# Queries and keys of two head pairs split at full height with halves placed by DMA, and attention bias tiles loaded by query half

## The chip, the core and the metric

The kernel runs on one core of a Trainium2 chip. A core has five engines that each work through their own list of instructions in order: TensorE (PE) for matrix products, VectorE (DVE), ScalarE (ACT) and GpSimd (POOL) for element-wise work, and SyncE (SP), which here only issues DMAs. They meet through semaphores. The metric is the device time of one execution in microseconds (us), the median of several runs.

## What is computed

Two layers of a diffusion backbone on 512 latent tokens (a grid of 8 rows by 64 columns) and 256 context tokens, model width 1024, everything in float32. Layer 0 has two groups of eight heads side by side: latent attention (MLA) and neighbourhood attention, then a SwiGLU block. Layer 1 has sliding-window attention and a SwiGLU block. The change concerns the neighbourhood heads of layer 0 alone. What they compute, cut to the core:

```python
def na_heads(q, k, v, qc, kc, vc, rel_bias, ctx_out):
    ...
    def row(args):
        r, qr = args
        rs = jnp.clip(r - kr // 2, 0, n_rows - kr)
        k_blk = lax.dynamic_slice_in_dim(kg, rs, kr, axis=1)[:, :, kcol]
        v_blk = lax.dynamic_slice_in_dim(vg, rs, kr, axis=1)[:, :, kcol]
        s_lat = jnp.einsum('bnqhd,bknmhd->bhnqkm', qr, k_blk).astype(jnp.float32) * scale
        s_lat = s_lat + col_bias[:, dr_idx].transpose(0, 2, 3, 1, 4)[None]
        s_lat = jnp.where(col_ok[:, :, None, :], s_lat, NEG_INF).reshape(b, h, n_cb, NA_CB, kr * NA_KB)
        s_ctx = jnp.einsum('bnqhd,bchd->bhnqc', qr, kc).astype(jnp.float32) * scale
        p = jax.nn.softmax(jnp.concatenate([s_ctx, s_lat], axis=-1), axis=-1).astype(v.dtype)
    ...
```

Each latent query reads the latent keys of a 16-column neighbourhood, with a learned bias, and all context keys, in one softmax; context queries read context keys.

## The kernel before

Activations lie transposed: features on the 128 partitions, the 768 tokens (512 latent, 256 context) along the free dimension. Two heads of width 64 share a tile, one in partitions 0 to 63 and one in 64 to 127; the eight neighbourhood heads are four such pairs, 0 to 3.

TensorE works in a rounded float32 type (fp32r). To keep full accuracy a value x is split into a high part, its cast to fp32r, and a low part, x minus the high part. For the scores (`stacked_scores`, L754) each head needs one query tile with the high part in one half of the partitions and the low part in the other, and two key tiles that hold the high part of the keys twice, and the low part twice. Two matmuls over all 128 partitions then give high times high plus low times high, and the rest.

`put_q` (L716) and `put_k` (L731) make these tiles. For pairs 0 and 1 they run straight out of the projection. For pairs 2 and 3 the projections first put the raw queries and keys into tiles of tag `p` (the list `raws`), and `split_pair` (L1032) makes the tiles later, as side work while pairs 0 and 1 are attended. For each of the two heads apart, on 64 partitions at a time: the query's high part is a cast (L723, on ScalarE), its low part a subtraction (L724, on GpSimd), which writes straight into the other half of the partitions; the keys' high part is a cast (L737, on VectorE for pair 2, on ScalarE for pair 3), the low part a subtraction on VectorE (L738), and a DMA copies each to the other half (L740 and L741, through the helper at L136). The tables `RK`, `RQ` and `RL` (L61) choose these engines. The tiles of pair 2 have tag `b`, those of pair 3 tag `st`.

The attention is a chain of jobs (`pair_jobs`, L637): for a pair first the context queries (blocks 4 and 5), then the latent query blocks 0 and 1 of both heads, then 2 and 3. In a job each head in turn has its scores made into a PSUM buffer of tag `s`, of which there are three; `take` (L567, VectorE) adds the bias, writes the negated scores to SBUF and keeps the extreme; `exps` (L563, ScalarE) takes the exponential and its sum. Then `turned` (L505 and on) transposes the probabilities on TensorE (L511), copies them out of PSUM (L502, VectorE, or L503, ScalarE), and `weighted` (L557) multiplies with the values. `attend` interleaves the front of one job with the back of the one before and with side work: the split, the norms of the MLA group (`gained`: squares on GpSimd L990, sums L997, roots L1000, gains on VectorE L977), later its projections (L346 to L349). While the first pair starts, VectorE, GpSimd and ScalarE still finish modulation sums (L240, L257, L258).

The bias of one head is two tiles of 128x768 of tag `nb`: tile 0 serves query blocks 0 and 1, tile 1 blocks 2 and 3. Tag `nb` has two buffers, so a third tile can be loaded only when the first is done with. `nb_tiles` (L953) issues both loads of a head when the pair's jobs are built, head after head.

The final order on each engine is made by a scheduler that simulates the program when it is built, with priorities from the order in which it is written. So an edit can move instructions around it. All DMAs named here are issued from SP, in one order: an issue that waits holds up those behind it.

## Time and profile before

| | |
|---|---|
| Timed runs | 1573.1, 1574.36, 1575.22 us; median 1574.36 |
| The profiled execution | 1578.6 us, its span 1576.8 |
| Mean granted TensorE clock | 0.993 |
| Neighbourhood attention begins, ends | about 177 us, about 262 us |

The profile follows one execution. Busy time counts what an engine executes; a wait is put down to what released it. `pss`, `pst`, `psd`, `pso` are PSUM tiles of the tags `s`, `t`, `d`, `o`. Where all DMAs of SP stand at L136, they are told apart by their tiles. Within the edited stretch the engines are busy as follows (us in each 20 us; the last three numbers are granted clock, share of the DMA engines, GB/s):

```profile
160.00:180.00 20.00, 19.45 (x117) 17.14 (x115) 15.64 (x35) 9.74 (x23) 13.19 (x11) 1.00 0.16 38
180.00:200.00 20.00, 17.57 (x121) 14.00 (x120) 15.23 (x39) 15.90 (x43) 13.66 (x9) 0.91 0.46 128
200.00:220.00 20.00, 17.93 (x131) 14.50 (x130) 15.23 (x40) 17.81 (x41) 4.63 (x5) 0.91 0.45 129
220.00:240.00 20.00, 19.50 (x150) 15.54 (x150) 15.86 (x37) 14.59 (x34) 7.45 (x5) 1.00 0.35 106
240.00:260.00 20.00, 19.53 (x150) 16.17 (x149) 16.24 (x40) 14.85 (x38) 9.57 (x8) 1.00 0.24 65
```

The columns are the stretch, its length, and the busy time of PE, of its weight loads, of DVE, ACT and POOL, each with its count of instructions.

### The profile page before, as it was taken

The numbers are of one execution on the slowest core, as the hardware profiler recorded it, in microseconds if no ns is written. First come the engines' busy times: TensorE is split into PE (matmuls) and PEld (weight loads), VectorE is DVE, ScalarE is ACT, GpSimd is POOL, SyncE is SP. The second block draws the span as 40 slices with busy tenths as digits, with TensorE's granted clock in tenths as the row PEclk, the third lists the DMA queues.
The fourth block names the chain that finished last, engine by engine and source line by source line (L and its number), as shares of the span: only waits on it lengthen the run. The fifth ranks groups of instructions, "written<-read, shape, count | busy, mean of one in ns | idle before, by whom it ended". The sixth has DMA issues, their size and how long they took to land.

```text
span 1576.8 us, 26525 instructions
## 1 busy us (share of the span) xinstructions
PE 1529.3 (97%) x10016; PEld 1372.7 (87%) x10016; DVE 1174.8 (75%) x2346; ACT 796.1 (50%) x1607; POOL 276.3 (18%) x302
## 2 busy tenths in 40 slices
PE   6999999999999999999999999999999999999998
PEld 4787778887998999999998988877889999899998
DVE  3885777685878587686858676879976778678685
ACT  4563677775465243242423335558856545354453
POOL 0144724320111101102111132470012000000001
PEclk9999999999999999999999999999999999999999
DMA  9645242004654444647466485110225133323322
GB/s 318 249 131 174 79 127 76 11 7 160 207 168 144 151 167 162 219 126 272 157 198 229 144 325 185 54 41 2 69 76 164 54 97 125 99 89 128 84 97 88
DMA packets 76463, 214.90 MB, mean 136 GB/s; under 512 B 9872, under 2 KB 16400, under 8 KB 76336
## 3 DMA queue, kind: packets, MB, share of 16 engines
q1 hardware_dynamic: 59216, 144.42, 28.1%
q0 software_dynamic: 15968, 67.24, 12.3%
q8 instruction: 78, 1.28, 0.3%
q10 hardware_dynamic: 1152, 1.57, 0.3%
q14 instruction: 49, 0.40, 0.1%
HBM read 186.97 MB, written 23.07 MB: 133 GB/s over the span
## 4 chain that ended last, share of the span: by engine, by line
PE 77%; DVE 10%; DMA 6%; ACT 3%; issue 2%; POOL 0%; SPq 0%; DVEq 0%; ACTq 0%; POOLq 0%
PE pso L557 5%; PE pss L1392 5%; PE pss L1391 5%; PE pss L1390 4%; PE psd L346 4%; PE psd L349 4%; PE psd L348 4%; PE pss L346 4%; PE pss L349 4%; PE pss L348 3%; PE pst L1392 3%; PE pst L1390 3%; PE pst L1391 3%; PE pst L346 3%; PE pst L348 3%; PE pst L349 3%
## 5 line engine op out<-in xcount | busy, mean ns | idle before, releaser
L335 ACT CAST wh<-wr 128x1024 fp32r<-128x1024 f32 (+2 forms) x148 | 115.5, 795 | 208.2 <-DMA wr<-in_w_dn_dram 48.9
L336 DVE TENSOR_TENSOR wl<-wr,wh 128x1024 fp32r<-128x1024 f32 (+2 forms) x145 | 133.0, 924 | 81.1 <-ACT wh L335 79.5
L563 ACT ACTIVATE p<-p,sm 128x512 f32<-128x512 f32 (+3 forms) x144 | 104.9, 729 | 28.5 <-DVE sm L567 26.7
L1390 PE MATMUL pss<-b,wh 128*128 128x384 f32 (+1 forms) x346 | 108.0, 313 | 0.6 <-ACT b L372 0.6
L1391 PE MATMUL pss<-b,wh 128*128 128x384 f32 (+1 forms) x346 | 108.2, 313 | 0.1
L1392 PE MATMUL pss<-b,wl 128*128 128x384 f32 (+1 forms) x346 | 107.3, 312 | 0.0
L348 PE MATMUL psd<-b,wh 128*128 128x512 f32 (+3 forms) x262 | 89.6, 342 | 0.0
L302 DVE CUSTOM_DVE_ANT_0 p<-rope,cond 128x1024 bf16<-128x1024 f32 x64 | 76.9, 1221 | 11.3 <-DMA rope<-in_mod_w_dram 11.2
L292 POOL DMA_DIRECT2D rope<-in_mod_w_dram x48 | 25.7, 535 | 321.1 <-DVE mod L302 308.7
L346 PE MATMUL psd<-b,wh 128*128 128x512 f32 (+3 forms) x222 | 80.0, 361 | 0.9 <-ACT b L476 0.6
L557 PE MATMUL pso<-ph,b 128*64 128x256 f32 (+1 forms) x384 | 78.9, 365 | 0.4 <-DVE ph L502 0.4
L349 PE MATMUL psd<-b,wl 128*128 128x512 f32 (+3 forms) x222 | 78.7, 355 | 0.0
L557 PE MATMUL pso<-pl,b 128*64 128x256 f32 (+1 forms) x384 | 78.5, 363 | 0.0
L1390 PE MATMUL pst<-b,wh 128*128 128x384 f32 (+1 forms) x226 | 70.7, 313 | 2.5 <-DVE p L1229 1.9
L1392 PE MATMUL pst<-b,wl 128*128 128x384 f32 (+1 forms) x226 | 70.7, 313 | 1.4 <-DVE wl L1378 1.4
L1391 PE MATMUL pst<-b,wh 128*128 128x384 f32 (+1 forms) x226 | 70.5, 312 | 0.0
L1377 ACT CAST wh<-pl 128x512 fp32r<-128x512 f32 x78 | 44.9, 620 | 50.0 <-PE pss L1391 22.6
L348 PE MATMUL pss<-b,wh 128*128 128x256 f32 (+3 forms) x216 | 69.2, 321 | 0.0
L1377 ACT CAST wh<-wr 128x1024 fp32r<-128x1024 f32 x39 | 41.0, 1051 | 54.5 <-PE pst L1391 14.6
L346 PE MATMUL pss<-st,wh 128*128 128x512 f32 (+2 forms) x198 | 67.1, 339 | 0.3 <-ACT wh L335 0.3
L349 PE MATMUL pss<-st,wl 128*128 128x512 f32 (+2 forms) x198 | 67.2, 339 | 0.1
L1390 PEld LDWEIGHTS pss<-b,wh 128*128 128x128 f32 x346 | 65.9, 191 | 1.1 <-ACT b L372 0.9
(627 smaller groups left out, 5377.6 us busy)
## 6 DMA issues: line engine op xcount, KB each, us to landing
wr<-in_w_gu_dram SPq DMA_DIRECT2D x88, 512.0 KB, 4.1
rope<-in_mod_w_dram POOLq DMA_DIRECT2D x48, 512.0 KB, 3.9
wr<-in_w_dn_dram SPq DMA_DIRECT2D x73, 256.0 KB, 3.0
wr<-in_w_out_dram SPq DMA_DIRECT2D x32, 512.0 KB, 4.0
p<-home POOLq DMA_DIRECT2D x40, 384.0 KB, 5.4
home<-p POOLq DMA_DIRECT2D x40, 384.0 KB, 5.4
wr<-in_w_in_dram SPq DMA_DIRECT2D x21, 512.0 KB, 4.4
nb<-in_nb_dram SPq DMA_DIRECT2D x16, 384.0 KB, 3.2
```

The source lines that it names most:

```text
L302: behind(V.tensor_tensor_reduce(out=T("p", [P, D], mybir.dt.bfloat16), in0=w, in1=cond[:, v, :], op0=ALU.mult, op1=ALU.add, scale=1.0, sca ...
L335: behind(S.copy(h, r), *after[:1])
L336: behind((G if eng else V).tensor_tensor(lo, r, f(h), op=ALU.subtract), *after[1:])
L346: ins = PE.matmul(o, wh[:, k], mh[:, c], start=first and k == 0, stop=False)
L348: PE.matmul(o, wh[:, k], ml[:, c], start=False, stop=False)
L349: PE.matmul(o, wl[:, k], mh[:, c], start=False, stop=last and k == n - 1)
L557: ins = PE.matmul(o[64 * i : 64 * i + 64, c], v(kt), t, start=n == 0, stop=n == len(moving[i]) - 1)
L563: S.activation(p[:, c], p[:, c], AF.Exp, bias=nm, scale=-1.0, accum_out=dn)
L1377: S.copy(h, t)
L1390: PE.matmul(o, wh, xh, start=first and k == 0, stop=False, skip_group_check=not first)
L1391: PE.matmul(o, wh, xl, start=False, stop=False, skip_group_check=not first)
L1392: PE.matmul(o, wl, xh, start=False, stop=k == 3, skip_group_check=not first)
```

## The change

Two edits. First, `split_pair` no longer calls `put_q` and `put_k`. The queries of both heads are cast in one instruction over all 128 partitions (ScalarE) and subtracted in one (VectorE, the low part written over the raw tile); the keys likewise. What has to lie in another half of the partitions is then placed by DMAs: three for the queries, six for the keys. Some of these overwrite what others read, so they wait for one another. Second, `nb_tiles` takes a pair and loads the tiles by query half: first head's tile 0, second head's tile 0, first head's tile 1, second head's tile 1.

```diff
-RK, RQ, RL, SQ = (2, 0), (0, 0), (0, 0), 1
+SQ = 1
...
-    def nb_tiles(h):
-        ts = [T("nb", [P, NT]) for i in range(2)]
+    def nb_tiles(p):
+        ts = {}
         for i in range(2):
-            dma(ts[i], I["nb"][h, i])
+            for s in range(2):
+                ts[s, i] = T("nb", [P, NT])
+                dma(ts[s, i], I["nb"][2 * p + s, i])
         cut = (slice(0, 512), slice(256, 768), slice(256, 768), slice(0, 512))
-        return lambda n: ts[n // 2][:, cut[n]]
+        return [lambda n, s=s: ts[s, n // 2][:, cut[n]] for s in range(2)]
...
-        how = S.copy, G.tensor_copy, V.tensor_copy
         sets.append((new_q(tag), new_k(tag)))
-        put_q(sets[p][0], None, how[RQ[p - 2]], (G, V)[RL[p - 2]].tensor_tensor)(q, slice(0, NT))
+        up, dn = slice(0, 64), slice(64, 128)
+        t0, t1 = sets[p][0]
+        S.copy(t0[:, :NT], q)
+        lo = q.bitcast(F32R)
+        V.tensor_tensor(lo, q, f(t0[:, :NT]), op=ALU.subtract)
         yield
-        put_k(sets[p][1], KC[1], how[RK[p - 2]])(k, slice(0, NT))
+        dma(t1[up, :NT], t0[dn, :NT])
+        dma(t1[dn, :NT], lo[dn])
+        dma(t0[dn, :NT], lo[up])
+        (h0, l0), (h1, l1) = sets[p][1]
+        S.copy(h0[:, :NT], k)
+        V.tensor_tensor(l0[:, :NT], k, f(h0[:, :NT]), op=ALU.subtract)
+        yield
+        for x, y in ((h0, h1), (l0, l1)):
+            dma(y[up, :NT], x[dn, :NT])
+            dma(y[dn, :NT], x[dn, :NT])
+            dma(x[dn, :NT], x[up, :NT])
         yield
...
-            hs = []
+            hs, near = [], nb_tiles(p)
...
-                hs.append(Head(..., None, nb_tiles(2 * p + s), -LOWEST, sums, mins))
+                hs.append(Head(..., None, near[s], -LOWEST, sums, mins))
```

In the built program GpSimd has four instructions fewer, VectorE and ScalarE two fewer each, SP ten DMAs more, and TensorE the same 9416 in a partly other order. Engine orders differ only between the start of the first pair's attention and the start of the MLA heads, and in one swap of neighbours far behind.

Where pair 2 is split, VectorE's order was this (L240 and L244 belong to a modulation sum; the `ISA` rows of L567 are takes, with `zeros` for context blocks and `nb` for bias tiles, and the row behind each reads its accumulator):

```order
L737 CAST b_1855<-p_1563 64x768
L240 ISA p_1786,mod_293_1376<-pl_1784,cond_66,mod_293_1376 128x512
L240 ISA mod_293_1376 128x1
L738 TENSOR_TENSOR b_1856<-p_1563,b_1855 64x768
L737 CAST b_1857<-p_1563 64x768
L244 SCALAR_TENSOR_TENSOR mod_293_1376<-mod_293_1376,modb_89 128x1
L567 ISA p_1834,sm_1824<-pss_1833,zeros_95 128x256
L567 ISA sm_1824 128x1
L567 ISA p_1844,sm_1824<-pss_1843,zeros_95 128x256
L567 ISA sm_1824 128x1
L738 TENSOR_TENSOR b_1858<-p_1563,b_1857 64x768
L567 ISA p_1876,sm_1824<-pss_1871,nb_1825 128x512
```

and with the change it is this (L1043 subtracts the queries, L1050 the keys):

```order
L240 ISA p_1786,mod_293_1376<-pl_1784,cond_66,mod_293_1376 128x512
L240 ISA mod_293_1376 128x1
L1043 TENSOR_TENSOR p_1478<-p_1478,b_1853 128x768
L244 SCALAR_TENSOR_TENSOR mod_293_1376<-mod_293_1376,modb_89 128x1
L1050 TENSOR_TENSOR b_1856<-p_1563,b_1855 128x768
L567 ISA p_1834,sm_1824<-pss_1833,zeros_95 128x256
L567 ISA sm_1824 128x1
L567 ISA p_1844,sm_1824<-pss_1843,zeros_95 128x256
L567 ISA sm_1824 128x1
L567 ISA p_1871,sm_1824<-pss_1866,nb_1825 128x512
```

Two instructions for four, and none is left between the context takes and the first bias take.

On SP, at the same place, four key copies stood ahead of the bias loads before. `nb_1829` is the first head's tile 1 afterwards and the second head's tile 0 before. A wait for a `DMAHW` counter is one for an earlier DMA:

```order
L136 DMA b_1855<-b_1855 64x768 [waits DMAHW5_49,DVE_49]
L136 DMA b_1856<-b_1856 64x768 [waits DMAHW6_49,DVE_49]
L136 DMA b_1857<-b_1857 64x768 [waits DMAHW7_49,DVE_49]
L136 DMA b_1858<-b_1858 64x768 [waits DMAHW0_49,DVE_49,PE_49]
L136 DMA nb_1829<-in_nb_dram 128x768 [waits DMAHW1_49,DVE_49]
L136 DMA nb_1830<-in_nb_dram 128x768 [waits DMAHW2_49,DMAHW1_49,DVE_49]
L136 DMA nb_2000<-in_nb_dram 128x768 [waits DMAHW3_49,DVE_49]
```

and with the change:

```order
L136 DMA b_1854<-b_1853 64x768 [waits DMAHW5_49,PE_49,Activation_49]
L136 DMA b_1857<-b_1855 64x768 [waits DMAHW6_49,PE_49,Activation_49]
L136 DMA b_1854<-p_1478 64x768 [waits DMAHW7_49,DVE_49]
L136 DMA b_1853<-p_1478 64x768 [waits DMAHW5_49,DMAHW0_49]
L136 DMA b_1857<-b_1855 64x768 [waits DMAHW1_49]
L136 DMA b_1858<-b_1856 64x768 [waits DMAHW2_49,DVE_49,PE_49]
L136 DMA b_1858<-b_1856 64x768 [waits DMAHW3_49]
L136 DMA b_1855<-b_1855 64x768 [waits DMAHW6_49,DMAHW4_49,DMAHW1_49]
L136 DMA nb_1829<-in_nb_dram 128x768 [waits DVE_49]
L136 DMA b_1856<-b_1856 64x768 [waits DMAHW3_49,DMAHW2_49]
L136 DMA nb_1831<-in_nb_dram 128x768 [waits DMAHW7_49,DVE_49]
```

Eight copies now stand ahead of the first bias reload, which is called A1 below, and one behind it; the fourth waits for the first, the eighth for the second and the fifth.

On ScalarE, behind the first context exponentials, the order with the change is this (L258 is a modulation sum, L503 a copy out of PSUM, L1041 the fourth pair's query cast; `p_1934` is the exponential that needs A1):

```order
L563 ACTIVATE p_1871,sm_1823<-p_1871,sm_1824 128x512
L563 ACTIVATE p_1834,sm_1823<-p_1834,sm_1824 128x256
L563 ACTIVATE p_1844,sm_1823<-p_1844,sm_1824 128x256
L258 ACTIVATE ph_1780,part_1801<-ph_1780 128x512
L563 ACTIVATE p_1895,sm_1823<-p_1895,sm_1824 128x512
L258 ACTIVATE pl_1784,part_1804<-pl_1784 128x512
L563 ACTIVATE wr_1913,sm_1823<-wr_1913,sm_1824 128x512
L563 ACTIVATE p_1924,sm_1823<-p_1924,sm_1824 128x512
L503 COPY ph_1886<-psd_1881 128x512
L1041 CAST st_2162<-p_1647 128x768
L563 ACTIVATE p_1934,sm_1823<-p_1934,sm_1824 128x512
```

Before, the first L258 stood ahead of the first of these rows, both PSUM copies ahead of the second head's exponentials, and between them and the exponential in the last row stood three casts.

## The prediction

> **What bounds the kernel now.** I read the page's first part, then the chain that ended last, then the stretches around the edited stage, then single instructions there. The page:

> ```profile
> span 1576.8 us, 26525 instructions
> PE 1529.3 (97%) x10016; PEld 1372.7 (87%) x10016; DVE 1174.8 (75%) x2346; ACT 796.1 (50%) x1607; POOL 276.3 (18%) x302
> PE 77%; DVE 10%; DMA 6%; ACT 3%; issue 2%; POOL 0%; SPq 0%; DVEq 0%; ACTq 0%; POOLq 0%
> ```

> TensorE is busy 97% of the span and carries 77% of the chain. No edit removes a matmul, so only time in which TensorE stands, or runs at a lower clock, can be won. The edits act between about 176 us (the first split) and about 260 us (the last bias tile). Busy time by stretch (columns: length, then PE, PEld, DVE, ACT, POOL; then the granted clock, DMA share, GB/s):

> ```profile
> 177.50:260.00 82.50, 76.47 (x558) 61.77 (x558) 64.96 (x159) 65.37 (x156) 37.69 (x28) 0.96 0.38 108
> 260.00:280.00 20.00, 20.00 (x153) 16.33 (x155) 12.83 (x39) 14.59 (x34) 7.02 (x8) 1.00 0.27 78
> ```

> TensorE stands for 82.50 - 76.47 = 6.0 us in this stretch, and behind it it is full again, so what is won there should be kept. The waits of that stretch (total, times, longest):

> ```profile
> PE pss L757 <- DVE sm L567: 3.0, 5, 0.9
> PE psd L511 <- DVE b L977: 1.5, 1, 1.5
> ```

> Half of it is score matmuls waiting for VectorE's `take` (L567) to free one of three PSUM buffers; a quarter is one wait for the gain multiplies. The clock adds to it:

> ```profile
> 182.00:184.00 2.00, 2.00 (x16) 2.00 (x16) 1.11 (x6) 2.00 (x7) 1.92 (x2) 0.84 0.45 98
> 184.00:186.00 2.00, 2.00 (x12) 2.00 (x11) 0.00 (x0) 0.93 (x4) 1.86 (x2) 0.50 0.63 194
> 186.00:188.00 2.00, 1.98 (x14) 1.68 (x14) 1.39 (x3) 0.77 (x2) 1.99 (x2) 0.80 0.01 3
> 214.00:216.00 2.00, 2.00 (x8) 1.21 (x8) 2.00 (x6) 2.00 (x5) 2.00 (x2) 0.52 0.00 2
> 216.00:218.00 2.00, 2.00 (x11) 1.34 (x10) 1.20 (x5) 2.00 (x6) 1.79 (x4) 0.62 0.54 133
> ```

> Twice the clock falls to half for about 3.4 us, each time right behind a group of waits. The first costs 2 x (0.16 + 0.50 + 0.20) = 1.7 us, the second 2 x (0.48 + 0.38) = 1.7 us. So the **most** that can be won is 6.0 + 3.4 = 9.4 us.

> **The split of the third pair.** VectorE and TensorE at its place:

> ```profile
> 176.74 1.14 DVE L738 TENSOR_TENSOR b<-p,b 64x768 fp32r<-64x768 f32 x1
> 177.91 0.65 DVE L737 CAST b<-p 64x768 fp32r<-64x768 f32 x1
> 178.58 0.24 DVE L244 SCALAR_TENSOR_TENSOR mod<-mod,modb 128x1 f32<-128x1 f32 x1
> 178.75 0.41 DVE L567 CUSTOM_DVE_ANT_0 p<-pss,zeros 128x256 f32<-128x256 f32 x1
> 179.54 1.45 DVE L738 TENSOR_TENSOR b<-p,b 64x768 fp32r<-64x768 f32 x1
> 181.02 0.69 DVE L567 CUSTOM_DVE_ANT_0 p<-pss,nb 128x512 f32<-128x512 f32 x1
> 179.22 0.39 PE L757 MATMUL pss<-st,st 128*128 128x256 f32 x1 [0.55 <-DVE sm L567]
> 180.10 0.33 PE L511 MATMUL pst<-ident_r,p 128*128 128x128 f32 x1
> 180.59 0.33 PE L511 MATMUL psd<-ident_r,p 128*128 128x128 f32 x1 [0.16 <-ACT p L563]
> 181.78 0.36 PE L757 MATMUL pss<-st,st 128*128 128x192 f32 x1 [0.85 <-DVE sm L567]
> ```

> The second subtraction (1.45 us) stands between the context takes and the first bias take; TensorE waits 0.85 us for that take, and 0.55 us for the one before. What the new operations cost follows from instructions of the same kinds and widths:

> ```profile
> 175.37 1.68 ACT L723 CAST b<-p 64x768 fp32r<-64x768 f32 x2
> 208.76 0.83 ACT L372 CAST b<-b 128x768 fp32r<-128x768 f32 x1
> L738 DVE TENSOR_TENSOR st<-p,st 64x768 fp32r<-64x768 f32 x2 | 1.9, 948 | 0.0
> 211.06 0.95 DVE L373 TENSOR_TENSOR b<-b,b 128x768 fp32r<-128x768 f32 x1
> L724 POOL TENSOR_TENSOR b<-p,b 64x768 fp32r<-64x768 f32 x2 | 4.2, 2116 | 0.2
> L724 POOL TENSOR_TENSOR st<-p,st 64x768 fp32r<-64x768 f32 x2 | 3.6, 1818 | 0.5 <-ACT st L723 0.4
> ```

> A cast of 128x768 takes 0.83 us, as one of 64x768 does (1.68 for two), and a subtraction 0.95 us at either height: twice the partitions are free. Third pair: VectorE loses two casts and two subtractions and gains two subtractions, ScalarE keeps two casts, GpSimd loses 4.2 us. Fourth pair: VectorE keeps two subtractions, ScalarE has two casts for four (1.7 us less), GpSimd loses 3.6 us. GpSimd's own time is worth nothing, since its later work (squares, weight splits) is waited for by nobody on the chain; but the two subtractions that ran beside it took 1.14 and 1.45 us, not 0.95.

> In the new order (shown with the change) both subtractions stand ahead of the first take, and nothing between the context takes and the bias take. ScalarE's casts end at 176.2 and 177.05, so the subtractions run 176.2 to 177.15 and, behind L244, 177.4 to 178.35. The first take starts at 178.35 instead of 178.75; two takes of 0.34 us later the bias take starts at 179.0 instead of 181.0 and ends at 179.7. The score matmul that waited until 181.78 then follows the transpose of 180.10 at 180.2: **1.6 us earlier**. The waits in that 3.4 us fall from 1.0 us to about 0.4, and I take it that the half clock behind them goes: **1.7 us**.

> [...]

> What is late next is ScalarE, whose exponentials the transposes need. Its prices:

> ```profile
> L563 ACT ACTIVATE p<-p,sm 128x512 f32<-128x512 f32 x7 | 5.0, 718 | 0.6 <-DVE sm L567 0.6
> L563 ACT ACTIVATION_READ_ACCUMULATOR p<-p,sm 128x1 f32 x14 | 2.6, 187 | 0.0
> L563 ACT ACTIVATE p<-p,sm 128x256 f32<-128x256 f32 x7 | 3.5, 496 | 0.0
> 192.91 0.72 ACT L563 ACTIVATE p<-p,sm 128x512 f32<-128x512 f32 x1
> 180.45 0.61 ACT L258 ACTIVATE ph<-ph 128x512 f32<-128x512 f32 x1
> 187.10 0.59 ACT L503 COPY ph<-psd 128x512 f32<-128x512 f32 x1 [2.18 <-PE psd L511]
> ```

> From 180.45 us, where the row of L258 begins now, the new order has four wide exponentials of 0.90 us, two narrow of 0.68, two sums of 0.80 (0.61 and its read), a copy of 0.59 and a cast of 0.83 ahead of the exponential that now starts at 192.91: 180.45 + 8.0 = 188.5, some 4.4 us earlier. So ScalarE covers 3.3 us, and the casts taken from the fourth pair leave it 1.7 us of slack.

> **The added DMAs.** The split now issues nine copies per pair where four stood, and the first pair's bias tile for its second query half (A1 below) is queued on SP behind eight of them. Landing times, of the whole program's SP transfers into or out of `b` in the last row:

> ```profile
> b<-b SPq DMA_DIRECT2D x4, 192.0 KB, 2.8
> nb<-in_nb_dram SPq DMA_DIRECT2D x4, 384.0 KB, 3.1
> DMA to landing us min/median/max: 2.0/3.3/8.2
> ```

> The fourth copy waits for the first to land (176.3 + 2.8 = 179.1), the eighth for the fifth (issued near 180.0, landed 182.8). A1 is issued near 183.3 and lands near 186.5. VectorE will be ready for its take at about 184, so it waits some 2.5 us, a wait that was not there; behind it on VectorE are queued one more take and two PSUM copies, for which TensorE waits, and on ScalarE the exponentials of both takes. But ScalarE reaches A1's exponential only at 188.5: 1.3 us of cover is left, and I price the wait at 0. Bounds: 0, and the 13.9 us of rival (d) if the copies pass one by one. The fourth pair's nine copies stand in the same way ahead of the second pair's tiles; the last of them waits for a subtraction some 4 us before those tiles come free, so I price them at 0 too, with the same upper bound.

> **The bias tiles.** Before, the second head's tile could be loaded only when the first head's was done with, right where it was needed; the chain runs through such loads:

> ```profile
> 202.07 2.95 DMA nb<-in_nb_dram
> 206.50 3.21 DMA nb<-in_nb_dram
> ```

> Now a load has the other head's two takes, near 1.4 us, and some copies as cover. But at the first of these ScalarE's square root, not the DMA, ended last, so I count only 0.5 us (bounds: 0, and 2.95 + 3.21 = 6.2 us if both loads leave the chain at full length). The 1.5 us wait for L977 and the half clock at 214 I leave, since the gain multiplies keep their place in VectorE's order.

> **Sum:** 1.6 + 1.7 + 0.5 = 3.8 us. The profiled execution took 1578.6 us (1576.8 of span and 1.8 around it), so 1574.8; it stands 4.2 us above the median of the timed runs, 1574.36, and from that the forecast is **1570.6 us**.

> **The rivals.** (a) Everything comes: the wait at 213 and its half clock also go, as the gain multiplies come earlier against TensorE. That adds 1.5 + 1.7, and of the 3.0 us of take waits the 1.6 us that are not named above may give another 1.0: -8.0, 1566.4. Against it: multiplies and transposes keep their order. [...] (c) ScalarE or VectorE holds TensorE back by what was won: 1574.4. (d) Slower: A1 lands late because the half-tile copies pass one after another. The eight ahead of it, at 2.8 us each from 176.2, put its issue at 198.6 and its landing at 201.7; its take has to start by 187.8 to be hidden, so 13.9 us are lost and 3.8 won: 1584.5. It decides once A1 lands 3.8 us behind that point, near 191.6. Against it: a full bias tile lands in 3.1 us, hardly longer than a half copy, and two of the copies wait for others, not eight. [...]

> **How the numbers follow.** Chances: forecast (2.5 to 5.5 us won) 0.45; (a) 0.15; (b) 0.18; (c) 0.12; (d) 0.10. 0.2% is 3.15 us, about what a measurement of this kernel can tell from no change. Faster by more: about 0.35 of the forecast and all of (a), 0.50. Slower: (d) and a little of (c), 0.11. Within: 0.39. The range runs from the 9.4 us bound, 1565.0, to 1.6 us above the median, 1576.0, and leaves (d) out.

> **What would show it.** Right: the first bias take begins about 2 us before 181.0; the wait of 0.85 us and the low clock at 183 to 187 are gone; GpSimd's L724 rows are gone; a VectorE wait for A1 of 2 to 3 us. Wrong: TensorE waiting over 1 us near 185 to 192, bias loads landing behind 188, or a half-clock stretch at a new place.

## The result, and the profile after

| | before | changed |
|---|---|---|
| Timed median, first session | 1575.48 us (15 runs) | 1571.22 us (15 runs) |
| Ratio, first session | | 0.9972, 95% interval 0.9963 to 0.9981 |
| Timed median, second session | 1573.65 us (25 runs) | 1570.73 us (12 runs) |
| Ratio, second session | | 0.998, 95% interval 0.9968 to 0.9991 |
| Span of the profiled execution | 1576.8 us | 1570.2 us |

The change makes the kernel faster by 4.3 us in the one session and 2.9 us in the other; the forecast was 3.8 us. The page of the changed kernel has, at its head and at the end of its chain of waits:

```profile
span 1570.2 us, 26531 instructions
PE 1526.4 (97%) x10016; PEld 1371.3 (87%) x10016; DVE 1175.1 (75%) x2344; ACT 793.5 (51%) x1605; POOL 267.5 (17%) x298
PE 80%; DVE 10%; DMA 4%; ACT 3%; issue 2%; POOL 0%; SPq 0%; DVEq 0%; ACTq 0%; POOLq 0%
```

TensorE still bounds it; DMA's share of the chain fell from 6% to 4%. The 6.6 us between the two spans must not be put down to the change. To see where it lies, I subtracted, for every n, the start of the n-th TensorE matmul in one trace from that in the other (all traces have 10016; the 9416 given with the change stands in none). At 176 us, ahead of the edited stage, the changed kernel is already 1.03 us ahead. The stage adds 2.5 us by 280 us, and that lead stays within 0.2 us up to 800 us. Then another 4 us come between 800 and 860 us, where the two orders are the same; a second profile of the kernel before gains those 4 us as well, so the first one was merely late there.

Busy time by stretch in the changed kernel (columns as in the prediction):

```profile
177.50:260.00 82.50, 75.20 (x578) 61.69 (x577) 65.92 (x161) 64.69 (x159) 30.84 (x26) 0.98 0.49 137
184.00:186.00 2.00, 1.16 (x11) 0.92 (x9) 0.29 (x3) 1.75 (x4) 0.00 (x0) 1.00 0.85 275
186.00:188.00 2.00, 1.38 (x10) 0.78 (x10) 2.00 (x6) 1.40 (x4) 0.00 (x0) 1.00 0.70 203
214.00:216.00 2.00, 2.00 (x21) 2.00 (x19) 2.00 (x6) 2.00 (x7) 1.02 (x3) 1.00 0.52 150
222.00:224.00 2.00, 0.22 (x2) 0.22 (x3) 1.97 (x4) 0.24 (x1) 0.58 (x1) 1.00 0.00 0
224.00:226.00 2.00, 2.00 (x12) 1.39 (x11) 2.00 (x6) 2.00 (x6) 0.00 (x0) 0.77 0.55 166
226.00:228.00 2.00, 2.00 (x7) 1.15 (x7) 1.73 (x5) 0.48 (x2) 0.00 (x0) 0.50 0.71 212
```

The half clock at 183 to 187 and at 214 to 218 is gone; a new stretch lies at 225. TensorE stands 7.3 us in the whole stretch, against 6.0 before, in new places. Its waits there:

```profile
PE pss L757 <- DVE sm L567: 4.8, 3, 2.4
PE psd L511 <- DVE b L979: 0.7, 1, 0.7
```

Three waits for `take` of up to 2.4 us stand where five of up to 0.9 us stood. Two of them matter. The first is at A1 (timelines of SP, VectorE, ScalarE and TensorE):

```profile
177.94 0.68 DVE L567 CUSTOM_DVE_ANT_0 p<-pss,nb 128x512 f32<-128x512 f32 x1
179.16 0.33 PE L757 MATMUL pss<-st,st 128*128 128x192 f32 x1
182.38 0.57 SPq L136 DMA_DIRECT2D nb<-in_nb_dram  x1
185.87 0.69 DVE L567 CUSTOM_DVE_ANT_0 p<-pss,nb 128x512 f32<-128x512 f32 x1 [1.67 <-DMA nb<-in_nb_dram]
186.60 0.72 ACT L563 ACTIVATE p<-p,sm 128x512 f32<-128x512 f32 x1 [0.85 <-DVE sm L567]
186.62 0.50 PE L757 MATMUL pss<-st,st 128*128 128x512 f32 x1 [1.46 <-DVE sm L567]
```

The first two rows are the gain at the split: the first bias take and the score matmul that waited for it have come from 181.02 and 181.78 to 177.94 and 179.16; without the 1.03 us from ahead of the stage, that is 2.05 and 1.59 us earlier. The last four rows are the price: the load of A1 keeps VectorE for 1.67 us, ScalarE for 0.85 and TensorE for 1.46.

The second is behind the latent operands' casts (L1132, line 1117 before), which nobody had touched:

```profile
218.41 1.53 POOL L336 TENSOR_TENSOR wl<-wr,wh 128x512 fp32r<-128x512 f32 x1 [3.28 <-ACT wh L335]
218.82 1.53 DVE L1132 CAST st<-b 32x768 fp32r<-32x768 f32 x1
220.00 2.57 POOL L336 TENSOR_TENSOR wl<-wr,wh 128x1024 fp32r<-128x1024 f32 x1
220.28 2.71 DVE L1132 CAST st<-b 32x768 fp32r<-32x768 f32 x1
223.02 0.69 DVE L567 CUSTOM_DVE_ANT_0 wr<-pss,nb 128x512 f32<-128x512 f32 x1
223.78 0.35 PE L757 MATMUL pss<-b,b 128*128 128x192 f32 x1 [2.37 <-DVE sm L567]
```

Each cast starts while GpSimd subtracts and ends some 0.4 us after GpSimd does: 1.53 and 2.71 us for what took 0.55 us in the kernel before:

```profile
225.01 0.55 DVE L1117 CAST st<-b 32x768 fp32r<-32x768 f32 x1
226.91 0.55 DVE L1117 CAST st<-b 32x768 fp32r<-32x768 f32 x1
227.57 2.38 POOL L336 TENSOR_TENSOR wl<-wr,wh 128x1024 fp32r<-128x1024 f32 x1 [5.54 <-ACT wh L335]
```

There the second cast was done 0.1 us before GpSimd began. Without the 1.03 us, the two casts now come 5.2 and 5.6 us earlier, and GpSimd's two subtractions 1.3 and 6.5 us, so that they meet; the take behind them is late, TensorE waits 2.37 us, and the half clock at 225 follows.

### The profile page after: what moved, and what is told of

Read it like the earlier page. It is cut to its first block, busy times and chain, and to the rows that moved or that the text cites. A ratio compares the mean times of both kernels' runs of the same rounds, so it can differ in the third digit from the quotient of the medians.

```text
span 1570.2 us, 26531 instructions
## 1 busy us (share of the span) xinstructions
PE 1526.4 (97%) x10016; PEld 1371.3 (87%) x10016; DVE 1175.1 (75%) x2344; ACT 793.5 (51%) x1605; POOL 267.5 (17%) x298
## 4 chain that ended last, share of the span: by engine, by line
PE 80%; DVE 10%; DMA 4%; ACT 3%; issue 2%; POOL 0%; SPq 0%; DVEq 0%; ACTq 0%; POOLq 0%
PE pso L557 5%; PE pss L1407 5%; PE pss L1406 5%; PE pss L1405 4%; PE psd L346 4%; PE pss L346 4%; PE pss L349 4%; PE pss L348 4%; PE psd L349 4%; PE psd L348 4%; PE pst L1407 3%; PE pst L1405 3%; PE pst L1406 3%; PE pst L346 3%; PE pst L349 3%; PE pst L348 3%
## 5 line engine op out<-in xcount | busy, mean ns | idle before, releaser
L563 ACT ACTIVATE p<-p,sm 128x512 f32<-128x512 f32 (+3 forms) x144 | 105.0, 730 | 27.3 <-DVE sm L567 24.9
## 6 DMA issues: line engine op xcount, KB each, us to landing
p<-home POOLq DMA_DIRECT2D x40, 384.0 KB, 5.4
home<-p POOLq DMA_DIRECT2D x40, 384.0 KB, 5.6
nb<-in_nb_dram SPq DMA_DIRECT2D x16, 384.0 KB, 3.3
```

The costliest lines, as they stand in the source:

```text
L563: S.activation(p[:, c], p[:, c], AF.Exp, bias=nm, scale=-1.0, accum_out=dn)
```

## The experiments

"Lead" is the difference of the n-th matmul's start to the first profile of the kernel before (the median over the nine matmuls from that time on), less what it was at 175 us; it shows one profiled execution. Between 180 and 284 us the orders of the matmuls differ, so that the n-th need not be the same one there. Leads at 190 are rough: the nine behind the changed kernel's 2.5 lie between 1.7 and 2.8. Ratios are to the kernel before on the same chip.

| kernel | median us (runs) | ratio, 95% interval | lead at 182 | at 190 | at 280 |
|---|---|---|---|---|---|
| before again | 1575.05 (12) | 1.0003, 0.999 to 1.0017 | -0.7 | -0.8 | -1.4 |
| changed (first profile) | 1571.22 (15) | 0.9972, 0.9963 to 0.9981 | 1.5 | 2.5 | 2.5 |
| changed again | 1570.73 (12) | 0.998, 0.9968 to 0.9991 | 1.5 | 2.3 | 3.1 |
| split only | 1571.16 (12) | 0.9984, 0.9972 to 0.9996 | 1.5 | 1.7 | 2.9 |
| bias order only | 1584.02 (6) | 1.0067, 1.0048 to 1.0086 | -2.0 | -1.2 | -2.1 |
| third pair only | 1570.58 (11) | 0.998, 0.9968 to 0.9992 | 1.5 | 2.4 | 3.6 |
| halves on VectorE | 1573.98 (12) | 1.0006, 0.9992 to 1.002 | -3.0 | -1.5 | -1.5 |
| casts on GpSimd | 1567.48 (6) | 0.9951, 0.9935 to 0.9966 | 1.5 | 2.7 | 5.0 |
| casts on ScalarE | 1568.1 (12) | 0.996, 0.9946 to 0.9974 | 1.5 | 2.4 | 6.4 |
| A1 from GpSimd | 1568.69 (8) | 0.997, 0.9958 to 0.9981 | 1.5 | 2.1 | 2.0 |
| casts and A1, GpSimd | 1567.11 (5) | 0.996, 0.9947 to 0.9972 | 1.5 | 2.1 | 4.2 |
| casts GpSimd, A1 ScalarE | 1570.4 (12) | 0.9979, 0.9968 to 0.9991 | 1.5 | 1.1 | 3.4 |
| casts GpSimd, copies behind A1 | 1567.9 (5) | 0.9961, 0.9946 to 0.9975 | 1.5 | 4.2 | 3.9 |

**The two controls.** The kernel before and the changed kernel, each unchanged.

> The kernel before, unchanged, as a control. Every theory expects a ratio of 1.000 within 0.001 to itself. It is run for its second profile and for the clock of each timed run. If the half-clock stretches of a profile (five of 3.4 us in the first profile of before, three in that of the changed kernel) come where the program makes them, this profile shows them at the same places, near 23, 183, 214, 846 and 1057 us. If they come by chance, some lie elsewhere, and the single runs differ by about 1.7 us for each stretch, that is for each 0.001 of mean clock.

> The changed kernel, unchanged, as a control and for a second profile. Ratio to the kernel before 0.9972 within its interval (0.9963 to 0.9981). If the program makes them, the waits of 1.46 us near 186 and of 2.37 us near 221 come again at the same places. If the half clock is set by where a fixed grid of time falls, the stretch at 225 may be elsewhere or missing though the wait ahead of it is there; if the wait alone sets it, the stretch comes again.

The kernel before, second profile, first a window, then TensorE's timeline at the split:

```profile
182.00:184.00 2.00, 2.00 (x12) 2.00 (x11) 0.70 (x2) 1.36 (x5) 1.92 (x2) 0.50 0.11 25
```

```profile
178.40 0.38 PE L757 MATMUL pss<-st,st 128*128 128x256 f32 x1 [0.55 <-DVE sm L567]
180.95 0.53 PE L757 MATMUL pss<-st,st 128*128 128x192 f32 x1 [0.85 <-DVE sm L567]
```

The waits of 0.55 and 0.85 us come again to the hundredth, and the half clock behind them too, here for twice as long (from 180.7 to 187.5, where it was 183.4 to 186.8). Both profiles of before also have one near 214; those near 23 and 846 of the first are missing in the second, which has one near 976 instead. In the changed kernel's second profile both new waits come again (TensorE's timeline), and neither is followed by half clock this time; a stretch lies at 212 instead (windows):

```profile
187.92 0.50 PE L757 MATMUL pss<-st,st 128*128 128x512 f32 x1 [1.65 <-DVE sm L567]
225.79 0.36 PE L757 MATMUL pss<-b,b 128*128 128x192 f32 x1 [1.50 <-DVE sm L567]
```

```profile
212.00:214.00 2.00, 2.00 (x10) 2.00 (x11) 2.00 (x7) 2.00 (x6) 2.00 (x1) 0.50 0.05 12
```

So the waits belong to the program, and the drops belong to them only loosely.

**Each half of the change alone.** Split only puts the old bias loop into the changed kernel, as below; bias order only puts the new one into the kernel before.

```diff
-    def nb_tiles(p):
-        ts = {}
...
+    def nb_tiles(h):
+        ts = [T("nb", [P, NT]) for i in range(2)]
+        for i in range(2):
+            dma(ts[i], I["nb"][h, i])
```

> The changed kernel with the bias tiles loaded per head as before, the split on all partitions kept. The forecast's theory: 3.3 us off the kernel before, ratio 0.9979, the first bias take again near 178 to 179 us and no half clock at 183. Rival (the bias order brings it): ratio within 0.0005 of 1.000. A third theory (the two need each other, since the earlier takes only help if the next tile is there): both single parts within 1 us of before.

> The kernel before with the bias tiles taken by query half, and the split left as it was. The forecast's theory (the split brings 1.6 + 1.7 us, the bias order 0.5 us): 0.5 us off the kernel before, ratio 0.9997, the 0.85 us wait for the first bias take still there near 182. Rival (the bias order brings most of it, since its loads leave the chain): 3 to 4 us, ratio 0.9977.

Split only gets the whole 1.5 us at 182, and 2.9 us at 280; its ratio, 0.9984, is 0.4 to 1.2 thousandths above the changed kernel's two, within the intervals. So the split carries most of the gain, as forecast (3.3 of 3.8), and it does so without the bias order. What that adds on top, 0.6 to 1.9 us by these ratios, the runs don't settle; it can be nothing.

Bias order only is 10 us slower than before, which no theory had. At its split, VectorE's small L244 and the second subtraction are held up, and TensorE waits two to three times as long for the same takes (timelines of both engines):

```profile
178.51 1.11 DVE L244 SCALAR_TENSOR_TENSOR mod<-mod,modb 128x1 f32<-128x1 f32 x1
180.01 0.38 PE L757 MATMUL pss<-st,st 128*128 128x256 f32 x1 [1.65 <-DVE sm L567]
183.09 0.36 PE L757 MATMUL pss<-st,st 128*128 128x192 f32 x1 [1.63 <-DVE sm L567]
399.54 0.44 PE L346 MATMUL pss<-st,wh 128*128 128x384 f32 x1 [1.85 <-ACT st L1182]
```

L244 took 1.11 us for 0.24 before, L738 1.98 for 1.45, both beside GpSimd's instructions. But the edit also makes the scheduler order the instructions differently up to 410 us, far behind the stage, and 3.4 us of its lead are lost between 280 and 400 us (the last row is one such wait). Its timed runs also have a lower mean granted clock, 0.9912 for 0.9936 of the kernel before in the same session, as much as two more stretches of 3.41 us at half clock, 3.8 us. It is no clean test of the bias order, and part of its 10 us stays open.

**The third pair only.** The fourth pair is split in two halves of 64 partitions as before.

```diff
+        if p == 3:
+            put_q(sets[p][0], None, S.copy, G.tensor_tensor)(q, slice(0, NT))
+            yield
+            put_k(sets[p][1], KC[1], S.copy)(k, slice(0, NT))
+            yield
+            return
```

> The changed kernel with the fourth pair's queries and keys split in halves as before; third pair and bias order as in the change. The forecast's theory (the gain is made at the third pair's split, the fourth pair's is worth nothing): ratio 0.9972 as the changed kernel. Rival (the fourth pair's shorter work on ScalarE and GpSimd, 1.7 and 3.6 us, is what carries it): 1.5 us or more slower than the changed kernel, 0.998 or more. Second rival (the fourth pair's nine copies cost something on SP): faster than the changed kernel by 1 us or more.

0.998 beside 0.998 for the changed kernel in the same session: the gain is made at the third pair's split, and the fourth pair's casts, copies and GpSimd time are worth nothing that can be measured, which here means less than about 2 us.

**Halves on VectorE.** The third pair's two subtractions (the queries' is shown) are cut in two, which puts 1.9 us back ahead of the first take.

```diff
-        V.tensor_tensor(lo, q, f(t0[:, :NT]), op=ALU.subtract)
+        for r in (up, dn) if p == 2 else (slice(0, P),):
+            V.tensor_tensor(lo[r], q[r], f(t0[r, :NT]), op=ALU.subtract)
...
```

> The changed kernel with the third pair's two subtractions each made in two halves of 64 partitions on VectorE, which adds two subtractions of about 0.95 us, 1.9 us in all, ahead of the first take; the casts and everything else of the change stay, though the scheduler moves some transposes. The forecast's first term (VectorE's work ahead of the first bias take holds up TensorE one for one): that take comes 1.9 us later against the split's start than in the changed kernel, the score matmuls wait about 1.5 to 1.9 us more by 182 us, and if that is kept the ratio is 0.998 + 0.0011 = 0.999. Rival (ScalarE's exponentials, for which TensorE waits 0.5 us there, now set the pace): no more than 0.5 us is lost by 190 us, ratio 0.998.

```profile
177.76 1.86 POOL L257 TENSOR_TENSOR ph<-ph,cond 128x512 f32<-128x512 f32 x1
178.53 1.12 DVE L244 SCALAR_TENSOR_TENSOR mod<-mod,modb 128x1 f32<-128x1 f32 x1
179.57 2.88 DVE L1052 TENSOR_TENSOR b<-p,b 64x768 fp32r<-64x768 f32 x2
182.48 0.42 DVE L567 CUSTOM_DVE_ANT_0 p<-pss,zeros 128x256 f32<-128x256 f32 x1
182.96 0.58 PE L757 MATMUL pss<-st,st 128*128 128x256 f32 x1 [4.09 <-DVE sm L567]
```

TensorE loses 4.5 us at 182 against the changed kernel. The first take comes 4.0 us later than there (182.48 for 177.26, less the 1.23 us by which all of this execution is behind at 175), and TensorE waits 4.09 us for it, where the changed kernel has no such wait. So lateness of the take is passed on one for one, and the rival (ScalarE sets the pace) falls. Only 1.9 of the 4.0 us are the added subtractions' own time: beside GpSimd's multiplies (L257) the later two took 1.44 us each for 0.95, and the one-element L244 1.12 for 0.35 in the changed kernel. The ratio is 1.0006; the 0.0026 to the changed kernel's 0.998, measured in another session, are 4.1 us, and the whole gain of the change is gone. Some of that is half clock: the mean granted clock of its timed runs is 0.9923, for 0.9945 there.

**The casts.** The four casts of L1132 move off VectorE, to GpSimd as below or to ScalarE.

```diff
-                    V.tensor_copy(KA[s][i][ROPE[s]], KR[i][:32])
+                    G.tensor_copy(KA[s][i][ROPE[s]], KR[i][:32])
```

> The changed kernel with the four casts of 32x768 (L1132) moved from VectorE to GpSimd; the scheduler moves some neighbours too. Theory A (two of these casts run beside GpSimd's weight subtraction, take 4.17 us for 1.10, hold up the next bias take, and so make TensorE's 2.37 us wait at 221.4 and the half clock behind it): both go, 2.4 + 1.7 = up to 4.1 us off the changed kernel, ratio to the kernel before 0.9946. Theory B (the wait would come anyway, by the next thing that is late, the exponentials or a bias load): as the changed kernel, ratio 0.9972, with a wait of 1.5 us or more near 220 to 228.

> The changed kernel with the four casts of L1132 on ScalarE instead of VectorE. Theory A (what costs 2.4 us and often a half-clock stretch near 221 is that VectorE's casts and GpSimd's weight subtraction run at the same time): the wait near 221 goes here too, ratio 0.995 to 0.996 as with the casts on GpSimd. Theory B (the casts on GpSimd won because the scheduler moved the neighbours): about the changed kernel, 0.997 to 0.998. ScalarE gets some 4 x 0.6 us more, so up to 1 us may be lost to later exponentials.

With the casts on GpSimd, where one takes 0.8 to 1.0 us, the window in which TensorE stood:

```profile
222.00:224.00 2.00, 2.00 (x15) 1.41 (x13) 2.00 (x6) 1.90 (x6) 0.97 (x1) 1.00 0.72 204
```

TensorE no longer waits there, between 222 and 224 as shown, and keeps the full clock there, with the casts on GpSimd as on ScalarE, where one takes 0.83 us; in the profile with GpSimd a stretch of half clock lies at 209 instead. Ratios of 0.9951 and 0.996 against 0.9972 and 0.998: theory A holds, with about 2 to 4.5 us won on top of the change. Two different engines and two different orders give it, which speaks against an accident of the order (theory B).

**A1.** The one load is issued from another queue, GpSimd's as below or ScalarE's:

```diff
-                dma(ts[s, i], I["nb"][2 * p + s, i])
+                dma(ts[s, i], I["nb"][2 * p + s, i], G if (p, i, s) == (0, 1, 0) else None)
```

Or, with the casts on GpSimd, the third pair's copies of keys are put behind it on SP:

```diff
+                if (p, i) == (0, 1):
+                    A1.append(ld)
...
-            dma(y[up, :NT], x[dn, :NT])
+            behind(dma(y[up, :NT], x[dn, :NT]), *A1)
...
```

> The changed kernel with one bias load alone, the first pair's tile for the second query half of its first head (A1), issued from GpSimd's queue ahead of three of its multiplies, not from SP's behind eight copies. Theory (the queue makes A1 late: its buffer is free at 181.4, SP issues it at 182.4): A1 is issued near 181.0, VectorE's wait of 1.67 us falls to about 0.3, TensorE's of 1.46 us at 185 to 187 goes; 1.0 to 1.5 us off the changed kernel at 195 us of the trace, ratio to the kernel before 0.9963 if it is kept to the end. Rival (VectorE waits for the load's own time of 3.5 us, whoever issues it): no difference.

> The changed kernel with both: the four casts of L1132 on GpSimd and A1 issued from GpSimd's queue. If the two waits add up: 7.7 us less than the kernel before for the casts and 1.0 to 1.5 us more for A1, ratio 0.9942. If the time won at A1 is given back at the next late operation before 215 us: as the casts alone, 0.9951.

> The changed kernel with the four casts of L1132 on GpSimd and the bias load A1 issued from ScalarE's queue. If the load's issue time is what matters: issued 1.25 us earlier than from SP behind the copies, it lands 1 us earlier in the order of work, TensorE's wait near 186 falls from about 1.5 to 0.5 us, and the ratio is 0.995 - 0.0006 = 0.9945. If the load's own time sets it (issued from GpSimd 1.25 us earlier it took 4.8 us for 3.5 and landed no earlier): the wait stays over 1.2 us, ratio 0.995 to 0.996.

> The changed kernel with the four casts of L1132 on GpSimd and the third pair's six copies of keys put on SP's queue behind the first pair's two bias loads for the second query half; their tiles are needed only some 25 us later. Theory (A1's landing is set by the copies that share the DMA engines with it: from three queues, issued up to 1.25 us apart, it landed within 0.4 us in the order of work): with six of nine copies out of the way, A1 is issued near 181 and lands in about 3.2 us, TensorE's wait near 186 (1.3 to 2.1 us in the four kernels) falls below 0.6, and the ratio is 0.9951 - 0.0007 = 0.9944. Rival (the load takes its 3.5 us or more for another reason, or the scheduler's new order of VectorE there costs what is won): the wait stays over 1.2 us, ratio 0.995 or more.

From the timelines and the rows of DMA issues (the last but one column puts the landing on the changed kernel's time, by the leads at 175 us):

| A1 issued by | at | to landing | landed | on one time | TensorE's wait |
|---|---|---|---|---|---|
| SP, behind eight copies (changed kernel) | 182.38 | 3.2 | 185.6 | 185.6 | 1.46 |
| GpSimd | 180.36 | 4.8 | 185.2 | 185.9 | 1.93 |
| ScalarE, casts on GpSimd | 180.46 | 5.1 | 185.6 | 186.0 | 2.12 |
| SP, ahead of six copies, casts on GpSimd | 180.91 | 2.8 | 183.7 | 183.7 | none |

From another queue it is issued 1.25 to 1.5 us earlier on one time and lands no earlier. The copies are in flight there: from 180 to 181 us in the run with GpSimd's queue, and from 180.2 to 181 in that with ScalarE's, the packets of SP's queue (q1) took 90% and 93% of the time of the 16 DMA engines, and none from 180.5 to 181.4 in the run with six of the nine copies out of A1's way. Only in that run does it land 1.9 us earlier; then the wait near 186 is gone and the lead at 190 is 4.2 us for 2.7. By 280 us that is given back, as the rival had it: the scheduler's new order has new waits (TensorE's timeline), and the ratio is 0.9961, not the 0.9944 expected:

```profile
205.47 0.49 PE L757 MATMUL pss<-st,st 128*128 128x512 f32 x1 [1.59 <-DVE sm L567]
219.82 0.40 PE L557 MATMUL pso<-ph,b 128*64 128x256 f32 x1 [1.30 <-DVE ph L502]
```

With A1 on GpSimd, VectorE had no wait for A1: its take follows a late addition, which stood beside two of GpSimd's multiplies (timelines of both):

```profile
182.39 1.47 POOL L992 TENSOR_TENSOR b<-b 128x768 f32<-128x768 f32 x1
183.82 1.47 POOL L992 TENSOR_TENSOR b<-b 128x768 f32<-128x768 f32 x1
182.40 2.92 DVE L260 TENSOR_TENSOR mod<-part,part 128x1 f32<-128x1 f32 x1 [0.46 <-ACT pl L258]
```

An addition of one element per partition, 0.28 us in the kernel before, takes 2.92 us: it began within 0.01 us of a GpSimd multiply and ended 0.03 us behind the end of the next one. Moving a load onto GpSimd had put its three multiplies 2.1 us later.

None of the three runs with A1 on another queue is faster than its like with A1 on SP beyond the intervals: 0.997 beside 0.998 with the casts on VectorE, and, with the casts on GpSimd, 0.996 from GpSimd's queue and 0.9979 from ScalarE's beside 0.9951. In the last, half clock follows the wait of 2.12 us, from 187.3 us, and the lead at 280 is 3.4 us for 5.0; the rest of its 4.4 us is open.

The four kernels with the casts off VectorE, and A1 not on ScalarE, lie at 0.9951 to 0.9961. That is below both ratios of the changed kernel, though their intervals touch its own; among themselves the runs don't order them.

## Why the prediction came out

- **Term 1 (takes come earlier, 1.6 us): right in size and cause.** The score matmul of 181.78 came 1.59 us earlier, and at 182 us the lead is 1.5 us in every kernel with the full-height split of the third pair. Undoing it on VectorE alone made the take late and took the whole gain away.
- **Term 2 (the half clock at 183 goes, 1.7 us): the drop went, but the reason given isn't shown.** Both profiles of before drop there. None of the seven profiles with the undivided split and A1 on SP does (two of the changed kernel, five of variants). But the prediction has it go because the waits there become shorter. On the grid of 3.41 us on which such stretches start (last section), TensorE stood for 1.05 and 1.35 us in the interval ahead of the drop in the two profiles of before; in the changed kernel's two it stands for 1.46 and 1.64 us in the interval around 186, and no drop follows. Why it went is open, and that this term came out is luck as far as its reason goes. The second stretch, at 214, was to stay; one stretch did stay, at 225 or at 212. Over the timed runs of the second session the mean granted clock is 0.9934 before and 0.9945 after (0.9941 after in the first; other sets of runs of the kernel before have 0.9929 to 0.9936). One stretch of 3.41 us at half rate costs 3.41 x 0.5 / 1570 = 0.0011 of it, so on average about one stretch less, 1.7 us, as forecast.
- **Term 3 (bias loads have cover, 0.5 us): not settled.** The runs allow 0.6 to 1.9 us on top of the split, with intervals wider than that.
- **A1 priced at 0: the step that failed.** Issue and landing were right: forecast 183.3 and 186.5 in before's time, measured 182.38 and 185.6, which is 183.4 and 186.6 with the 1.03 us by which this execution is ahead. VectorE was ready at 185.2 in that time, not 184, and waited 1.67 us, not 2.5. But the 1.3 us of cover wasn't there, for two reasons. TensorE did not wait for the exponential but for the take itself, which has to free a PSUM buffer for the next scores. And the sum for ScalarE added each exponential's own time and that of its read, 0.90 us, where the two overlap and one exponential follows the other after 0.71 us (ScalarE's timeline of the changed kernel):

```profile
183.04 0.71 ACT L563 ACTIVATE wr<-wr,sm 128x512 f32<-128x512 f32 x1
183.66 0.18 ACT L563 ACTIVATION_READ_ACCUMULATOR wr<-wr,sm 128x1 f32 x1
183.75 0.71 ACT L563 ACTIVATE p<-p,sm 128x512 f32<-128x512 f32 x1
```

  So ScalarE was ready at 186.8 in before's time, not 188.5. Price: 1.46 and 1.65 us of TensorE in the two profiles.
- **The fourth pair at 0: right** to within about 2 us, by the run with the third pair alone.
- **What was not in the sum:** the casts that meet GpSimd's subtractions, 1.50 to 2.37 us of TensorE's time, and in one profile a half-clock stretch. The prediction priced GpSimd's time at nothing, since nobody waits for its results; but VectorE's two casts took 1.53 and 2.71 us for 0.55 beside its subtractions. It had seen that two subtractions beside GpSimd took 1.14 and 1.45 us for 0.95, but didn't ask where else VectorE and GpSimd would meet once their work had moved.

The sum came out, but in part by luck. From 175 us to 300 us, where all these orders agree again, the same matmuls take 125.0 and 126.4 us in the two profiles of before, and 122.5 and 121.9 in the two of the changed kernel. TensorE stands longer in that stretch, not shorter: 7.3 and 6.6 us for 6.0 and 6.2, since the two omissions cost more than the earlier takes save. Half clock costs 1.7 us in each, for 3.4 and 5.1. The rest, the busy time at full clock, is 113.5 us in both, for 115.6 and 115.1: 1.6 to 2.1 us which no term of the sum had, and which stood in for what the omissions took. The profile models where a matmul ends, so short waits may be hidden in busy time; where these 2 us come from is open. Two of the prediction's own signs of being wrong came true, too: TensorE waited over 1 us at 185 to 187, and half clock lay at a new place, 225; the stretch at 214, which the forecast left in place, went.

Rival (d), slower, fell by its size: the copies do hold up A1, but by 1.9 us and not 13.9. One after another, as rival (d) took them, the eight would have put A1's issue 22.4 us behind the first copy (eight times 2.8); SP issued the first at 175.20 and A1 at 182.38, 7.2 us behind. From the other two queues A1 landed 0.3 and 0.4 us later.

The rows of L1132, L244 and L260 are alike: each is a VectorE instruction that began beside one of GpSimd and outlasted it. L244 (1.12 us with the halves on VectorE, for 0.35 in the changed kernel) ended 0.03 us behind a GpSimd multiply, the two casts of L1132 (1.53 and 2.71 us for 0.55) 0.4 us behind a subtraction each, and L260 (2.92 us for 0.28) 0.03 us behind the second of two multiplies. What couples the two engines isn't shown.

## What to carry to other kernels

Ahead of an engine that bounds the kernel, count what stands in front of its supplier's first instruction: here two more subtractions on VectorE made its first take 4.0 us late, half of it by their own time and the rest while GpSimd worked beside VectorE, and TensorE waited 4.1 us for it, while what the fourth pair's split was spared on ScalarE and GpSimd was worth nothing measurable. Whenever a change moves VectorE's work in time, lay its timeline beside GpSimd's: two casts that met GpSimd's subtractions cost 1.5 to 2.4 us of waiting, and moving the four to another engine brought 2 to 4.5 us, about as much as the change itself. A load issued into a burst of copies landed 0.3 and 0.4 us later from two other queues, and 1.9 us earlier with six of the nine copies put behind it; and cover is measured from start to start, not by adding durations that overlap.

## What the runs showed of the hardware

Near 972 us in nine profiles, and near 192 in two, a stretch follows an interval with less than 0.5 us of idle time on record. In these intervals TensorE works through matmuls with a single column: 24 of L398 (128x1) took 2.73 us in the changed kernel, 12 of L999 took 1.40. Counted as idle time, they bring the nine intervals to 1.94 to 2.43 us and the two to 1.64; in the five profiles with no stretch near 972, no interval there comes to more than 1.78 us. No run changes these matmuls, so whether they have to do with the half clock there isn't shown. Two stretches that follow another at once, behind 0.25 and 0.76 us counted so, stay open.
